# Layer 0's first modulation group: four of its eight steps on TensorE in front of the statistics of x

## The chip, the core and the metric

The kernel runs on one core of a Trainium2 chip. A core has TensorE (PE; its weight loads are listed as PEld), VectorE (DVE), ScalarE (ACT), GpSimd (POOL) and SyncE (SP), which issues most transfers. Each engine takes its own queue of instructions in order and waits on semaphores for the others. The time is the device time of one execution in microseconds, the median of three runs; a profiler's record of one more execution gives the rows below.

## The reference

One inference step of a two-layer backbone (`DEPTH = 2`, model width 1024) for 128 context tokens and 512 latent tokens. Each layer computes a modulation vector from a conditioning vector (one for the context, one for the latent tokens), normalises and modulates x, runs four parallel head groups (gated convolution, chunked spatial gating, latent attention, windowed attention), projects, adds through a gate, and then does the same around a squared-ReLU MLP:

```
mod = silu(c) @ w_ada[l] + b_ada[l]          # six vectors of 1024: shift1, scale1, gate1, shift2, scale2, gate2
h   = rmsnorm(x, norm1) * (1 + scale1) + shift1
y   = mixer(h);  x = x + gate1 * y
x   = x + gate2 * (relu(rmsnorm(x, norm2) * (1 + scale2) + shift2) @ w1) ** 2 @ w2
```

where rmsnorm divides x by the root of its mean square over the 1024 channels. The outputs are the final normed tokens and the context's keys and values of each layer.

## The kernel before, in words

All tokens (640) lie together, channels on partitions: x is one tile of 128 x 8 x 640, block k holding channels 128k to 128k + 127. Weights come from memory as `raw` tiles, and ACT and DVE split each into a high and a low part (`load_unit`: ACT copies L239, DVE subtracts L240, output `hl`). The activations `h` are split likewise (L336, L337), and every product is three matmuls (`mm3`, L248 to L250). The first product is that of `tm_block` (tokens on partitions, weights `in_wt`, PSUM tiles `tm`).

The part in question is `first_modulate`, which makes layer 0's first `h`. Its pieces:

- `broadcast_c` (L159, L161): PE and ACT spread the conditioning vectors `cs` over all partitions into `cb`.
- `norm.start()`: ACT squares x block by block (L266, L269), DVE adds the squares into `ss` (L270). Then `rstd` for each half of the tokens (384 and 256): PE sums over partitions (L290), DVE scales and adds epsilon into `nst` (L293), POOL raises to the power -0.5 (L295), PE spreads the result over the partitions (L297, tile `rb`), ACT copies it to `rbs` (L281).
- The modulation of shift1 and scale1 in natural layout, by `AdaRows`: the first group covers channel blocks 0 to 3 and has eight steps, k = 0 to 7. A step is a transfer of 512 KB (`adan`, from `in_wnat`, L311) and two matmuls of 512 columns onto two rows (`adar`, L198). `finish` copies the rows (ACT, `adas`, L205), transposes them (PE, `adat`, L210) and adds the bias (DVE, `mod`, L213; gains L184). A second group covers blocks 4 and 5 (L327, four transfers from `in_wnat2`, matmuls of 256 columns).
- `ada_tile` for blocks 6 and 7, and for all later modulation vectors: a transfer `adaw` (L171) and two multiply-and-sum instructions on DVE (L174, one with output `junk`, one with output `adaw`).
- DVE multiplies x by `rbs` into `xr` (L319), ACT applies gains and shifts (L334) and copies the high part of `h` (L336), DVE subtracts for the low part (L337).

The tile framework lowers this to one queue for each engine. Within an engine it is free to order instructions by its own estimates of when each is ready and by the program's order as a priority; it also hands out the buffers of a pool by these estimates, so that an `adaw` or `adan` tile can stand in a buffer that an earlier one held, and its transfer then waits for the reader of the earlier one. Layer constants that `layer` asks for at its start are drawn forward into the front: the masks (`wide`, L440, cast to `msk`, L442), a row of norms and sinks (`row`, L444) and from it `nsink` (L446). The first weight splits of `tm_block` are drawn forward too.

Of the kernel before, what the change touches and what calls it, by code (L numbers as in the profile page):

```python
# [56 lines left out]
def step_kernel(ctx, tc, xT, wf, wt, wt3, wo1, wo2, wq, wkvs, wada, wnat, wnat2, vec, rows, fnorm, cvec, cache, kpec,  # L57
# [44 lines left out]
    def ta(shape, s, dt=F32R):  # L102
        return pool_a.tile(shape, dt, tag="a", name=nm(s))

    def tb(shape, s, dt=F32R):
        return pool_b.tile(shape, dt, tag="b", name=nm(s))

    def tp(shape, s):
        return pool_p.tile(shape, F32, tag="p", name=nm(s))
# [10 lines left out]
    def f(ap):  # L120
        return ap.bitcast(F32)
# [20 lines left out]
    def late_consts():  # L142
        nc.sync.dma_start(out=vecs[1], in_=vec[1])
        nc.sync.dma_start(out=fn, in_=fnorm)
# [8 lines left out]
    def broadcast_c():  # L153
        for g in range(2):
            for j in range(2):
                ps = bank("cb")
                for i in range(4):
                    k = 4 * j + i
                    nc.tensor.matmul(ps[:, 128 * i:128 * (i + 1)], lhsT=cs[:, g, k:k + 1].to_broadcast([128, 128]),  # L159
                                     rhs=ident, start=True, stop=True)  # L160
                nc.scalar.copy(cb[:, g, 512 * j:512 * (j + 1)], ps)  # L161
# [6 lines left out]
    def ada_tile(l, ct, pool=None):  # L168

        raw = pool([128, D], "adaw", F32) if pool else rawp.tile([128, D], F32, tag="raw", name=nm("adaw"))  # L170
        nc.sync.dma_start(out=raw, in_=wada[l, ct])  # L171
        junk = bank2("junk").rearrange("p a b -> p (a b)")
        for g in range(2):
            nc.vector.tensor_tensor_reduce(  # L174
                out=raw if g else junk, in0=raw, in1=cb[:, g, :], op0=ALU.mult, op1=ALU.add, scale=1.0,
                scalar=vecs[l][:, V_BADA + ct:V_BADA + ct + 1], accum_out=mods[l][g][:, ct:ct + 1])
        v, k = divmod(ct, KT)
        if v in (1, 4):
            gain(l, v // 4, k, 1)
# [122 lines left out]
    def first_modulate():  # L302

        h = [ta([128, 2, TOK], "h") for _ in range(KT)]
        ar = AdaRows(0, 4)
        norm = Norm()
        broadcast_c()
        norm.start()
        for k in range(KT):
            raw = (tb if k % 2 == 0 or k >= 6 else tt)([128, D], "adan", F32)  # L310
            nc.sync.dma_start(out=raw, in_=wnat[k])  # L311
            ar.step(k, raw)
        ts = [None] * KT
        for i in range(3):
            two = ta([128, 2, TOK], "xr", F32)
            ts[2 * i], ts[2 * i + 1] = two[:, 0, :], two[:, 1, :]
        ts[6], ts[7] = tp([128, TOK], "xr"), tp([128, TOK], "xr")
        for k in range(KT):
            nc.vector.tensor_mul(ts[k], x[:, k, :], norm.rb)  # L319
        ar.finish()  # L320
        for k in (6, 7):
            ada_tile(0, k, tb)
            ada_tile(0, KT + k, tb)
        ar = AdaRows(4, 2)
        for k in range(0, KT, 2):
            raw = tb([128, 2, 512], "adan", F32)
            nc.sync.dma_start(out=raw, in_=wnat2[:, k:k + 2, :])  # L327
            for i in range(2):
                ar.step(k + i, raw[:, i, :])
        ar.finish()  # L330
        for k in K_FIRST:
            t = ts[k]
            for t0, n, g in ((0, LAT, 0), (LAT, CTX, 1)):
                nc.scalar.activation(t[:, t0:t0 + n], t[:, t0:t0 + n], AF.Identity,  # L334
                                     scale=gains[0][g][0][:, k:k + 1], bias=mods[0][g][:, k:k + 1])
            nc.scalar.copy(h[k][:, 0, :], t)  # L336
            nc.vector.tensor_sub(h[k][:, 1, :], t, f(h[k][:, 0, :]))  # L337
        late_consts()
        return h
# [994 lines left out]

    open_phase("mix0", lay=1, pt=3)
    h = first_modulate()
    for l in range(DEPTH):
        if l:
            open_phase(f"mix{l}", lay=1, pt=3)
        norm = Norm()  # L1340
# [147 lines left out]
```

## Time and profile before

| what | value |
|---|---|
| median of 3 runs | 1513.88 us (1511.9 to 1515.99) |
| the profiled execution's own time | 1513.0 us |
| its span | 1510.8 us |
| PE busy | 1461.8 us, 97% |
| DVE busy | 1133.2 us, 75% |
| ACT busy | 694.7 us, 46% |
| first `tm` matmul | 46.74 us after the span's start |

Times in the rows are counted from the span's start. A row with "[5.89 <-DMA row<-in_rows]" says that the engine stood 5.89 us before it, and what released it. The span is 2.2 us shorter than the execution's time. Two successive records of an `adar` matmul of 512 columns belong to one instruction, and so do two records of a `cb` or `rb` matmul.

### The profile page before, as it was taken

Reading aid. Unit: us, or ns where it says so; the run is one execution under the profiler, and the core shown is the slowest. Engines: PE = TensorE matmul, PEld = TensorE weight load, DVE = VectorE, ACT = ScalarE, POOL = GpSimd, SP = SyncE. Lnnn points to the kernel's source line nnn. Section 1 sums busy time; section 2 is a strip of 40 time slices with the busy share of each in tenths; the row PEclk is TensorE's granted clock in tenths of the full one; section 3 lists DMA queues with packets and bytes.
Section 4 is the critical chain, followed back from the end, with each engine's and each line's share of the span. In section 5 each row is a group of like instructions: output and inputs, shape, how many; then the busy total and the mean of one; then the engine's idle time right before and its main releaser. Section 6 shows DMA issues by size and latency. Waiting matters only on the chain.

```text
span 1510.8 us, 24974 instructions
## 1 busy us (share of the span) xinstructions
PE 1461.8 (97%) x9700; PEld 1405.1 (93%) x9700; DVE 1133.2 (75%) x2297; ACT 694.7 (46%) x1469; POOL 79.3 (5%) x103
## 2 busy tenths in 40 slices
PE   6999999999999999999999999999999999999997
PEld 3898989899999999999999998998999999999996
DVE  5998888889977867875477676887977666567656
ACT  4644556746233232233246455775826334324431
POOL 0011102200000000000000121110000000000000
PEclk9999999999999999999999999999999999999998
DMA  9643311324655444443112411022123123222312
GB/s 346 205 153 127 96 56 58 96 87 153 194 161 161 155 144 150 153 153 127 64 49 75 134 43 44 22 71 67 57 78 104 57 84 98 70 70 85 96 45 71
DMA packets 50422, 160.87 MB, mean 106 GB/s; under 512 B 6272, under 2 KB 10368, under 8 KB 50304
## 3 DMA queue, kind: packets, MB, share of 16 engines
q1 hardware_dynamic: 48320, 154.68, 31.8%
q10 hardware_dynamic: 1664, 3.93, 0.7%
q8 instruction: 77, 1.26, 0.3%
q0 software_dynamic: 320, 0.66, 0.2%
q14 instruction: 41, 0.34, 0.1%
HBM read 155.55 MB, written 3.05 MB: 105 GB/s over the span
## 4 chain that ended last, share of the span: by engine, by line
PE 81%; DVE 8%; ACT 5%; issue 2%; POOL 1%; DMA 1%; POOLq 0%; DVEq 0%; ACTq 0%
PE w L250 15%; PE w L249 15%; PE w L248 14%; PE tm L250 2%; PE tm L248 2%; PE tm L249 2%; PE qcd L248 2%; PE qcd L250 2%; PE qcd L249 2%; PE out L248 2%; PE fm L248 2%; PE fm L250 2%; PE fm L249 2%; PE out L249 2%; PE out L250 2%
## 5 line engine op out<-in xcount | busy, mean ns | idle before, releaser
L248 PE MATMUL w<-u,hl 128*128 128x384 f32 (+1 forms) x1024 | 315.8, 309 | 1.9 <-DVE x L428 1.2
L249 PE MATMUL w<-u,hl 128*128 128x384 f32 (+1 forms) x1024 | 315.9, 308 | 0.7 <-DVE u L1231 0.7
L250 PE MATMUL w<-u,hl 128*128 128x384 f32 (+1 forms) x1024 | 315.5, 309 | 0.6 <-DVE hl L240 0.6
L239 ACT CAST hl<-raw 128x1024 fp32r<-128x1024 f32 (+3 forms) x176 | 170.7, 972 | 244.0 <-PE w L250 151.4
L240 DVE TENSOR_TENSOR hl<-raw,hl 128x1024 fp32r<-128x1024 f32 (+3 forms) x176 | 199.4, 1135 | 60.6 <-ACT hl L239 59.8
L428 DVE SCALAR_TENSOR_TENSOR x<-w,mod,x 128x128 f32<-128x128 f32 (+1 forms) x384 | 155.4, 434 | 59.4 <-PE w L250 58.1
L248 PEld LDWEIGHTS w<-u,hl 128*128 128x128 f32 x1024 | 193.3, 189 | 3.0 <-DVE x L428 1.4
L249 PEld LDWEIGHTS w<-u,hl 128*128 128x128 f32 x1024 | 193.6, 189 | 1.0 <-DVE u L1231 1.0
L250 PEld LDWEIGHTS w<-u,hl 128*128 128x128 f32 x1024 | 193.4, 189 | 0.8 <-DVE hl L240 0.8
L249 PE MATMUL w<-h,hl 128*128 128x384 f32 (+1 forms) x576 | 178.8, 311 | 0.7 <-DVE h L369 0.6
L248 PE MATMUL w<-h,hl 128*128 128x384 f32 (+1 forms) x576 | 177.8, 311 | 0.4 <-ACT h L365 0.2
L250 PE MATMUL w<-h,hl 128*128 128x384 f32 (+1 forms) x576 | 178.1, 310 | 0.0
L174 DVE CUSTOM_DVE_ANT_0 junk<-adaw,cb,vec 128x1024 f32<-128x1024 f32 x84 | 108.2, 1289 | 30.6 <-DMA adaw<-in_wada 30.5
L249 PEld LDWEIGHTS w<-h,hl 128*128 128x128 f32 x576 | 109.8, 191 | 1.7 <-DVE h L369 1.5
L248 PEld LDWEIGHTS w<-h,hl 128*128 128x128 f32 x576 | 109.6, 191 | 1.4 <-ACT h L365 1.3
L250 PEld LDWEIGHTS w<-h,hl 128*128 128x128 f32 x576 | 109.8, 191 | 0.2
L174 DVE CUSTOM_DVE_ANT_0 adaw<-adaw,cb,vec 128x1024 f32<-128x1024 f32 x84 | 107.9, 1285 | 0.7
L248 PE MATMUL fm<-h,hl 128*128 128x256 f32 (+1 forms) x288 | 91.5, 318 | 0.0
L249 PE MATMUL fm<-h,hl 128*128 128x256 f32 (+1 forms) x288 | 89.7, 311 | 0.0
L250 PE MATMUL fm<-h,hl 128*128 128x256 f32 (+1 forms) x288 | 89.5, 311 | 0.0
L1176 ACT ACTIVATE rr<-w 128x384 f32<-128x384 f32 (+1 forms) x72 | 31.4, 436 | 101.5 <-PE w L250 101.4
L249 PE MATMUL tm<-hl,h 128*128 128x384 f32 (+1 forms) x240 | 77.3, 322 | 0.6 <-DVE hl L240 0.6
(338 smaller groups left out, 3237.1 us busy)
## 6 DMA issues: line engine op xcount, KB each, us to landing
raw<-in_wf SPq DMA_DIRECT2D x146, 512.0 KB, 3.5
adaw<-in_wada SPq DMA_DIRECT2D x84, 512.0 KB, 3.6
raw<-in_wo SPq DMA_DIRECT2D x24, 384.0 KB, 3.1
adan<-in_wnat SPq DMA_DIRECT2D x12, 512.0 KB, 8.2
raw<-in_wt SPq DMA_DIRECT2D x16, 384.0 KB, 4.0
x<-in_xT ACTq DMA_DIRECT2D x4, 640.0 KB, 7.1
raw<-in_wt SPq DMA_DIRECT2D x8, 288.0 KB, 2.8
raw<-in_wo SPq DMA_DIRECT2D x4, 512.0 KB, 3.6
```

Of the source, the lines that this page charges most:

```text
L174: nc.vector.tensor_tensor_reduce(out=raw if g else junk, in0=raw, in1=cb[:, g, :], op0=ALU.mult, op1=ALU.add, scale=1.0, scalar=vecs[l][:, ...
L239: nc.scalar.copy(hl[:, 0, :n], raw[:, :n])
L240: nc.vector.tensor_sub(hl[:, 1, :n], raw[:, :n], f(hl[:, 0, :n]))
L248: nc.tensor.matmul(out, lhsT=lhs[0], rhs=rhs[0], start=start, stop=False, skip_group_check=more)
L249: nc.tensor.matmul(out, lhsT=lhs[0], rhs=rhs[1], start=False, stop=False, skip_group_check=more)
L250: nc.tensor.matmul(out, lhsT=lhs[1], rhs=rhs[0], start=False, stop=stop, skip_group_check=more)
L428: nc.vector.scalar_tensor_tensor(out=x[:, m, t0:t0 + n], in0=ps[:, t0 - b0:t0 - b0 + n], scalar=mods[l][g][:, gate + m:gate + m + 1], in1= ...
L1176: nc.scalar.activation(r, ps[:, :n], AF.Relu)
```

## The change

The start of the statistics moves from in front of the loop over the first group's eight steps to the place between its fourth and its fifth step. Nothing else is edited; from L308 on every line has a number that is higher by one.

```
         broadcast_c()
-        norm.start()
         for k in range(KT):
+            if k == 4:
+                norm.start()
             raw = (tb if k % 2 == 0 or k >= 6 else tt)([128, D], "adan", F32)
             nc.sync.dma_start(out=raw, in_=wnat[k])
             ar.step(k, raw)
```

The order on PE, from behind `cb` to the transposes, with the lines of before (-) and of after (+). Two matmuls onto `adar_138` are one step of the first group; `rb` L290 are the sums over partitions and `rb` L297 the spreading, once for each half:

```order
-L290 MATMUL rb_209<-ones,ss_139 128x1 x3
-L290 MATMUL rb_220<-ones,ss_139 128x1 x2
-L297 MATMUL rb_209<-ident,nst_213 128x128 x3
-L297 MATMUL rb_220<-ident,nst_223 128x128 x2
-L198 MATMUL adar_138<-adan_229,cs 2x512 x2
+L198 MATMUL adar_138<-adan_176,cs 2x512 x2
+L290 MATMUL rb_225<-ones,ss_139 128x1 x3
+L198 MATMUL adar_138<-adan_245,cs 2x512
+L297 MATMUL rb_225<-ident,nst_229 128x128 x3
+L198 MATMUL adar_138<-adan_245,cs 2x512
+L290 MATMUL rb_236<-ones,ss_139 128x1 x2
+L198 MATMUL adar_138<-adan_249,cs 2x512
```

Before, the statistics stand in front of all eight steps; now four steps stand in front of the sums (the fourth is shown), and the matmuls of steps 4 and 5 stand between the pieces of the statistics.

On DVE, from the last sum of squares on, before. `nst` are the statistics, `xr` the products of x and `rbs`, `hl` the low part of a weight split, `msk` the masks:

```order
L270 TENSOR_TENSOR ss_139<-ss_139,sq_205 128x256
L293 TENSOR_SCALAR nst_213<-rb_209 128x3
L293 TENSOR_SCALAR nst_223<-rb_220 128x2
L446 TENSOR_SCALAR nsink_390<-row_388 128x4
L319 TENSOR_TENSOR xr_261<-x,rbs_208 128x640 x2
```

and after:

```order
L270 TENSOR_TENSOR ss_139<-ss_139,sq_221 128x256
L447 TENSOR_SCALAR nsink_390<-row_388 128x4
L240 TENSOR_TENSOR hl_405<-raw_403,hl_405 128x768
L293 TENSOR_SCALAR nst_229<-rb_225 128x3
L443 CAST msk_386<-wide_384 128x768
L293 TENSOR_SCALAR nst_239<-rb_236 128x2
L240 TENSOR_TENSOR hl_410<-raw_408,hl_410 128x768
L320 TENSOR_TENSOR xr_261<-x,rbs_224 128x640 x2
```

Both `nst` now stand behind `nsink` and the first `hl`, the cast of the masks stands between them, and a second `hl` in front of the first `xr`.

On SP, from the first weights on, with the lines of before (-) and of after (+); `raw` are the weights of `tm_block`, `adaw` the transfers of `ada_tile`, `wide` the masks:

```order
 L237 DMA raw_80_403<-in_wt 128x768
+L171 DMA adaw_51_294<-in_wada 128x1024
+L441 DMA wide_65_384<-in_masks 128x768
+L171 DMA adaw_53_301<-in_wada 128x1024
 L237 DMA raw_82_408<-in_wt 128x768
 L237 DMA raw_84_413<-in_wt 128x768
-L1097 DMA kx_347_2187<-in_rope_q 128x640
-L171 DMA adaw_51_294<-in_wada 128x1024
-L440 DMA wide_65_384<-in_masks 128x768
-L171 DMA adaw_53_301<-in_wada 128x1024
```

Up to the first weights the queue is the same; behind them two `adaw` and the masks go in front of the second and third weights. From the first `tm` matmul on, the order on PE is the same in both programs.

## Rows read from the trace of the kernel before

**Rows 1.** The page, part 1: engine, busy us, share, instructions.
```profile
PE 1461.8 (97%) x9700; PEld 1405.1 (93%) x9700; DVE 1133.2 (75%) x2297; ACT 694.7 (46%) x1469; POOL 79.3 (5%) x103
```

**Rows 2.** Windows: stretch, length, busy us by engine, granted clock, DMA share, GB/s.
```profile
core 0: us, PE busy (x) PEld busy (x) DVE busy (x) ACT busy (x) POOL busy (x), PEclk, DMA share, GB/s
11.50:15.20 3.70, 0.01 (x1) 0.00 (x0) 2.40 (x7) 3.09 (x8) 0.00 (x0) 1.00 1.02 407
17.00:23.40 6.40, 6.01 (x15) 2.81 (x16) 0.76 (x2) 0.85 (x2) 1.02 (x2) 0.50 1.02 371
22.60:46.00 23.40, 20.93 (x69) 5.38 (x67) 22.76 (x43) 11.10 (x18) 0.00 (x0) 0.98 0.96 348
46.00:60.00 14.00, 13.62 (x78) 13.16 (x79) 14.00 (x28) 8.90 (x19) 0.00 (x0) 1.00 0.45 149
60.00:100.00 40.00, 40.00 (x253) 40.00 (x252) 38.44 (x84) 21.89 (x73) 4.45 (x4) 1.00 0.53 169
```

**Rows 3.** The chain that ended last, 0 to 47 us: start, length, what.
```profile
31.59 5.16 DMA adan<-in_wnat
...
36.79 1.46 PE adar L198 x6
...
40.43 5.17 ACT xr L334 x9
...
46.74 0.44 PE tm L248
```

**Rows 4.** Waits of PE, 46 to 110 us: total, times, longest.
```profile
PE adat L210 <- ACT adas L205: 0.8, 1, 0.8
PE sgu L248 <- DVE u L609: 0.5, 1, 0.5
PE tm L248 <- ACT h L336: 0.2, 1, 0.2
```

**Rows 5.** Timeline of the front: start, length, engine, line, tiles, count, idle before.
```profile
5.58 5.93 PE L159 MATMUL cb<-ident,cs 128*128 128x128 f32 x32 [5.58 <-DVE cs L151]
...
15.28 1.28 PE L290 MATMUL rb<-ones,ss 128*128 128x1 f32 x10 [3.77 <-DVE ss L270]
...
16.14 0.16 DVE L293 TENSOR_SCALAR nst<-rb 128x3 f32<-128x3 f32 x1 [0.58 <-PE rb L290]
...
17.39 2.50 PE L297 MATMUL rb<-ident,nst 128*128 128x128 f32 x10 [0.84 <-POOL nst L295]
...
19.82 15.79 PE L198 MATMUL adar<-adan,cs 128*2 128x512 f32 x32
19.93 0.37 ACT L281 COPY rbs<-rb 128x256 f32<-128x256 f32 x1 [0.38 <-PE rb L297]
...
22.64 0.17 DVE L446 TENSOR_SCALAR nsink<-row 128x4 f32<-128x4 f32 x1 [5.89 <-DMA row<-in_rows]
22.72 5.97 DVE L319 TENSOR_TENSOR xr<-x,rbs 128x640 f32<-128x640 f32 x8
...
23.76 0.83 ACT L239 CAST hl<-raw 128x768 fp32r<-128x768 f32 x1 [3.46 <-DMA raw<-in_wt]
...
29.81 0.55 DVE L442 CAST msk<-wide 128x768 bf16<-128x768 f32 x1
...
32.69 0.95 DVE L240 TENSOR_TENSOR hl<-raw,hl 128x768 fp32r<-128x768 f32 x1
...
36.98 1.27 DVE L174 CUSTOM_DVE_ANT_0 adaw<-adaw,cb,vec 128x1024 f32<-128x1024 f32 x1
...
19.82 3.58 PE L198 MATMUL adar<-adan,cs 128*2 128x512 f32 x4
```

**Rows 6.** Transfers: first and fourth of the group, all weights: KB, us to landing.
```profile
adan<-in_wnat SPq DMA_DIRECT2D x1, 512.0 KB, 7.4
4.93 0.33 SPq L311 DMA_DIRECT2D adan<-in_wnat  x1
adan<-in_wnat SPq DMA_DIRECT2D x1, 512.0 KB, 10.0
raw<-in_wf SPq DMA_DIRECT2D x146, 512.0 KB, 3.5
```

More of the change, by code (lines that the diff above doesn't have):

```diff
@@ L307, in first_modulate @@
         broadcast_c()
-        norm.start()
         for k in range(KT):
+            if k == 4:
+                norm.start()
             raw = (tb if k % 2 == 0 or k >= 6 else tt)([128, D], "adan", F32)
```

## The prediction, made before the result was known

> **What bounds the kernel now.** I read the page first: TensorE (PE) is busy 97% of the span and VectorE (DVE) 75% [rows 1]. So a change at the start is worth what it does to the moment at which PE gets its steady work, and to what PE waits for after that. The windows of the front come next: in [rows 2] the reader is to see that DVE is busy 22.76 of 23.40 us from 22.6 to 46.0, all of 46 to 60, and 38.44 of 40.00 us from 60 to 100, while PE is full as well. From 22.6 to 100 us both engines are loaded, and DVE has 0.6 + 0 + 1.6 us left. The chain of waits [rows 3] goes through the second modulation group's transfer, `adar`, and the modulation on ScalarE (ACT) to the first token matmul `tm` at 46.74. And the waits of PE after that [rows 4] hold one wait of 0.5 us for DVE (at the `sgu` matmuls): at about 109 us DVE has no lead over PE. A DVE that falls behind in the front is therefore paid for by PE before 110 us.
>
> The timeline [rows 5] gives the front in order. PE spreads `cs` into `cb` (ends 5.58 + 5.93 = 11.51), then has nothing until `ss` is summed (15.28). The statistics run through DVE `nst`, GpSimd `nst` and PE L297 and end in `rbs` at 19.93 + 0.37 = 20.3. The eight steps of the first group take PE from 19.82 to 35.61. DVE has its `nst` done early (16.14), then stands until `row` lands (22.64), and starts the `xr` multiplies at 22.72; from there it hardly pauses.
>
> **The change part by part.** No operation is added or dropped: 16 `adar` matmuls, the same transfers, the same statistics. What moves is the order, and it moves on three engines.
>
> PE, the four steps. Two `adar` matmuls are one step, each leaves two records. Four records at the low clock took 3.58 us, so 1.79 a matmul; the other 28 took 15.79 - 3.58 = 12.21, so 0.87 a matmul [rows 5]. Eight of them behind `cb` are 7.0 us at the high clock: 11.5 to 18.5. The transfers don't stop them: the first lands at 1.64 + 7.4 = 9.0, the fourth at 4.93 + 10.0 = 14.9 [rows 6], and the fourth's turn is 11.5 + 5.2 = 16.7. Taken by itself this fills 3.8 us of PE's idle time and delays the column sums L290 from 15.28 to 18.5.
>
> DVE, the real cost. In the new order `nst` no longer stands directly behind the sums of `ss`. In front of it stand `nsink` and the first weight split `hl`, and between the two `nst` the cast of the masks; a second `hl` stands in front of `xr`. An engine takes its queue in order: [rows 5] show DVE passing nothing while `nsink` waits for `row`, though `rbs` was there from 20.3. Step by step:
> - `nsink` goes at 22.64, since `row` stands at the same place in SyncE's queue.
> - `hl` needs ACT's copy of the first weights, which starts when they land: 23.76 + 0.83 = 24.6. Then `hl` takes 0.95: 25.5. All of that is ahead of the first `nst`, which before ran at 16.14.
> - From `nst` to L297 it took 17.39 - 16.14 = 1.25, so L297 for half 0 starts at 26.8. Three matmuls: 5.93/16 = 0.37 each at the high clock, 2.50/5 = 0.50 at the low one; 27.9 or 28.3.
> - Behind them PE does the second matmul of step 4 (0.87 or 1.79), two column sums (1.28/5 each, 0.5), and half 1's `nst` follows some 0.2 later: 29.5 or 30.8. The masks are in by then: they and one 512 KB transfer stand behind the weights that land at 23.7, 0.92 MB at 0.41 MB a us [rows 2] are 2.2 us, so 25.9.
> - 1.25 later L297 for half 1 could start, 30.7 or 32.0; one `adar` matmul stands before it and ends at 30.2 or 32.4. Two matmuls and the copy to `rbs` (0.37): 31.9 or 33.8.
> So `xr` starts at 31.9 to 33.8 and not at 22.72: 9.2 to 11.1 us later. Of what DVE did later before, two `hl` and the mask cast are done by then, 2 x 0.95 + 0.55 = 2.45 us. DVE's lag on the same work is 6.7 to 8.6 us.
>
> The clock. In [rows 2] PE has nothing from 11.5 to 15.2 and is then granted 0.50 from 17.0 to 23.4, that is 1.2 GHz, before it returns to 2.4 GHz. After the change PE stands from about 19.9 to 26.8, longer than that, so I take the low clock as likelier for what follows 26.8. The Trainium skill, "TensorE: Matmul & The Clock Gate", section "HAM oscillation — how this bites in real kernels", says that a wait between two groups of matmuls re-throttles PE and the next group starts cold; by it the lag is the 8.6 above. Read the other way, that the four early steps keep PE warm, the lag would be 6.7. The trace agrees with the first for a shorter stop.
>
> ACT and the first `tm`. Eight `xr` take 5.97: 37.9 to 39.8. Behind them stand the transposed shift rows (0.24 in all), one modulation reduction (1.27) and the gains, so the first gains come at about 39.5 to 41.4 against 40.4 before, where ACT starts at 40.43 [rows 3]. Eight of ACT's nine pieces of 5.17 us: 44.1 to 46.0. ACT then wants the gains of channel block 6, five reductions of 1.27 behind the first gains: 45.9 to 47.8, then one piece of 0.5, the copy of the second group 0.5 and the cast of `h` 0.6: `tm` at 47.5 to 49.4, which is 0.8 to 2.7 later than 46.74. The rest of DVE's lag is not gone. It stands behind the front as weight splits and evictions that come later, and PE meets it before 110 us.
>
> What of the lag passes: DVE can shrink its 1.6 us of idle between 60 and 100 us. 6.7 - 1.6 = 5.1 and 8.6 - 1.6 = 7.0; I take the middle, 6.0. Its least is the start of `tm` alone (0.8), its most the whole 8.6 with nothing shrunk, or more if transfers come late (below). From about 110 us on the order on PE is the same as before, and PE is full, so what is lost stays lost.
>
> The sum: the profiled execution took 1513.0 us, its span 1510.8; 1513.0 + 6.0 = 1519.0. The median of the three runs is 1513.88, 0.9 above the profiled one, so I predict 1519.9.
>
> **The rivals.**
> Absorbed. The lag is real, but DVE catches up: only the start of `tm` passes, 0.8 to 2.7, which is 1514.7 to 1516.6. For it: PE waits for DVE only 0.5 us in all between 46 and 110 [rows 4], and much of what DVE does there are modulation vectors that are read only later. Against it: that work stands in DVE's queue in front of the splits that PE does read, and DVE has 1.6 us to give.
>
> Faster. The first group no longer stands behind the statistics. If `nst` ran at 18.5 + 0.9 = 19.4 (L290 to `nst` was 0.86), `rbs` would be there at about 23.5, `xr` would slip by under 1 us, PE would end the group with its remaining four steps at about 28 instead of 35.6, and the chain of [rows 3] would lose up to the 7 us between, less what DVE cannot follow: 1506.5 to 1512. It decides by one thing, whether the first `nst` starts before 20 us. Against it stands the DVE order itself: `hl` in front of `nst` cannot run before 24.6.
>
> Heavier. The third transfer of the second group goes into a buffer that its first transfer used, so it waits until PE has done that one's four matmuls. Step 6 ends at about 33.5 to 36; a landing takes 3.5 [rows 6] to 5.16 [rows 3]: 37 to 41. Four matmuls are half as wide as step matmuls, 4 x 0.44 = 1.8; the third transfer lands 3.5 to 5.2 later, 42.3 to 48, and eight matmuls of 0.44 end at 46 to 51.5. ACT's copy of this group stands in front of the casts of `h`; above it was wanted at 46.4 to 48.3. Up to 4 us come on top: 1522 to 1524.
>
> That the change does not do what it says is no rival: the order shows the steps in front.
>
> **How the numbers follow.** This kernel's measurement tells about 0.3% from no change, 4.5 us: faster is under 1509.3, slower over 1518.4. Forecast (lag passes but for DVE's idle time, 1517.9 to 1521): 0.60. Absorbed: 0.21. Heavier: 0.13. Faster: 0.06. The forecast's low end lies inside the 0.3%, 0.04 of it; so slower is 0.56 + 0.13 = 0.69, same 0.21 + 0.04 = 0.25, faster 0.06. The range goes from 1515.0, which leaves out the fast case and the lightest of the absorbed one, to 1523.5, which leaves out the worst of the heavy one.
>
> **What would show it.** Right: `nsink`, `hl`, then `nst` on DVE at 25.5; PE empty between about 20 and 26.8, a clock of 0.50 after it; `xr` from 32 to 34; `tm` 1 to 3 us later; and one wait of PE for DVE of 2 to 4 us between 60 and 110 us that before does not have. Wrong: an `nst` before 24 us; `xr` before 30; PE without a new wait for DVE behind `tm`; or a later start of `tm` by 5 us and more that is released by the second group's transfer.

## The result, and the profile after

| | median of the runs | runs | ratio to before, 95% interval |
|---|---|---|---|
| before | 1515.04 us (1511.9 to 1516.53) | 8 | |
| after | 1525.8 us (1520.26 to 1529.58) | 8 | 1.0075 [1.0059, 1.0091] |
| predicted | 1519.9 us (1515.0 to 1523.5) | | |

The change costs 0.0075 x 1515 = 11.4 us (8.9 to 13.8); the two medians differ by 10.8. The direction was forecast and the size was not: I took 6.0 us, and the median lies outside the range. The profiled execution of after took 1528.39 us, 2.6 over its median; its span is 1526.5.

The page of after, part 1, answers [rows 1]. The work of DVE is the same to 0.1 us, and PE has 6.6 us more, at a mean granted clock of 0.983 against 0.988:

```profile
PE 1468.4 (96%) x9700; PEld 1408.0 (92%) x9700; DVE 1133.1 (74%) x2297; ACT 694.3 (45%) x1469; POOL 80.3 (5%) x103
```

The windows of after, columns as in [rows 2]:

```profile
11.50:15.20 3.70, 3.70 (x20) 1.78 (x19) 2.40 (x6) 3.34 (x9) 0.00 (x0) 1.00 1.03 412
20.00:26.80 6.80, 1.63 (x8) 0.68 (x8) 1.24 (x4) 0.83 (x1) 0.27 (x1) 0.87 1.03 373
26.80:33.60 6.80, 6.14 (x15) 2.48 (x15) 1.56 (x3) 1.21 (x2) 1.97 (x2) 0.50 0.57 197
60.00:100.00 40.00, 37.67 (x218) 37.29 (x217) 38.24 (x81) 20.43 (x60) 2.78 (x3) 1.00 0.53 156
22.60:46.00 23.40, 16.36 (x52) 5.92 (x52) 13.55 (x25) 8.10 (x13) 2.24 (x2) 0.78 0.70 256
46.00:60.00 14.00, 10.35 (x47) 6.55 (x47) 11.15 (x25) 8.41 (x15) 0.00 (x0) 0.88 0.49 162
```

PE is full where it was empty (11.5 to 15.2), and then has 1.63 of 6.80 us from 20.0 on and a granted clock of 0.50 behind that, 1.2 GHz. DVE's busy time from 22.6 to 46 falls from 22.76 [rows 2] to 13.55, and from 46 to 60 from 14.00 to 11.15. The transfers thin out too: their share of the stretch from 22.6 to 46 falls from 0.96 to 0.70.

The front of after in order of time, as in [rows 5]:

```profile
19.85 0.83 PE L290 MATMUL rb<-ones,ss 128*128 128x1 f32 x6
...
23.50 0.17 DVE L447 TENSOR_SCALAR nsink<-row 128x4 f32<-128x4 f32 x1 [7.68 <-DMA row<-in_rows]
24.48 0.83 ACT L239 CAST hl<-raw 128x768 fp32r<-128x768 f32 x1 [9.29 <-DMA raw<-in_wt]
25.35 0.96 DVE L240 TENSOR_TENSOR hl<-raw,hl 128x768 fp32r<-128x768 f32 x1 [1.68 <-ACT hl L239]
26.22 0.15 DVE L293 TENSOR_SCALAR nst<-rb 128x3 f32<-128x3 f32 x1
...
27.46 1.65 PE L297 MATMUL rb<-ident,nst 128*128 128x128 f32 x6 [5.83 <-POOL nst L295]
29.04 1.87 PE L198 MATMUL adar<-adan,cs 128*2 128x512 f32 x2
...
30.84 1.02 PE L290 MATMUL rb<-ones,ss 128*128 128x1 f32 x4
...
31.78 1.87 PE L198 MATMUL adar<-adan,cs 128*2 128x512 f32 x2
31.89 0.16 DVE L293 TENSOR_SCALAR nst<-rb 128x2 f32<-128x2 f32 x1 [4.57 <-PE rb L290]
...
32.13 1.36 POOL L295 TENSOR_TENSOR nst<-nst,mhalf 128x2 f32<-128x2 f32 x1 [4.72 <-DVE nst L293]
...
33.58 1.22 PE L297 MATMUL rb<-ident,nst 128*128 128x128 f32 x4
...
35.24 5.97 DVE L320 TENSOR_TENSOR xr<-x,rbs 128x640 f32<-128x640 f32 x8 [2.32 <-ACT rbs L281]
...
48.81 5.30 PE L198 MATMUL adar<-adan,cs 128*2 128x256 f32 x16 [2.76 <-DMA adan<-in_wnat]
...
54.15 0.57 ACT L205 COPY adas<-adar 2x512 f32<-2x512 f32 x1 [4.61 <-PE adar L198]
...
55.22 0.17 DVE L213 TENSOR_TENSOR mod<-adat,vec 128x4 f32<-128x4 f32 x1 [2.85 <-PE adat L210]
...
55.40 0.44 PE L248 MATMUL tm<-hl,h 128*128 128x384 f32 x1 [0.22 <-DVE mod L213]
```

The sums over partitions are done at 20.7, and `nst` reads them at 26.22: in between DVE passes `nsink` and `hl`, which wait for transfers. `xr` starts 12.5 us later than at 22.72 [rows 5], and `tm` 8.66 later than at 46.74 [rows 3]. These are the longest of PE's waits from 46 to 125 us of after; in [rows 4] there are 1.5 us in all:

```profile
PE adar L198 <- DMA adan<-in_wnat: 2.8, 1, 2.8
PE tm L248 <- DVE mod L174: 2.3, 1, 2.3
PE sgu L248 <- DVE u L610: 1.0, 2, 0.6
```

The first lies in front of `tm`, the others behind it.

To see what is lost I take one and the same `sgu` matmul of layer 0 in every kernel, behind which waits for DVE add half a us at most: it runs at 106.30 us before and at 118.42 after, 12.1 later (8.7 of them up to `tm`; of the other 3.5, the last two waits above make 2.3 and, in the longer of the two for `u`, 0.6). The windows from 0 to it, first of before, then of after (third busy time is DVE's):

```profile
0.00:106.30 106.30, 93.25 (x498) 74.40 (x498) 87.26 (x183) 56.41 (x141) 7.59 (x14) 0.97 0.69 241
```

```profile
0.00:118.42 118.42, 96.69 (x498) 74.62 (x498) 87.19 (x182) 56.24 (x142) 8.56 (x14) 0.94 0.64 216
```

DVE has the same 87.2 us of work in both; it is idle 106.30 - 87.26 = 19.04 us before and 31.23 after. The 12.2 us between are the whole delay. This is a sum that comes out whatever the cause: on PE the same delay is 96.69 - 93.25 = 3.4 us more of busy time, at a lower clock, and 8.7 us more of idle time. Which engine sets the pace is told only by runs in which one of them is moved alone (below). DVE's waits say where they are: first of before, 15 to 106.3 us, then of after, 15 to 118.42 us (total, times, longest):

```profile
DVE nsink L446 <- DMA row<-in_rows: 5.9, 1, 5.9
DVE cq L499 <- POOL rstd L480: 1.0, 1, 1.0
DVE nst L293 <- PE rb L290: 0.9, 2, 0.6
DVE rstd L588 <- POOL rstd L480: 0.8, 1, 0.8
DVE ckp L536 <- POOL rstd L480: 0.7, 2, 0.4
DVE mod L213 <- PE adat L210: 0.6, 1, 0.6
DVE hl L240 <- ACT hl L239: 0.4, 1, 0.4
```

```profile
DVE nsink L447 <- DMA row<-in_rows: 7.7, 1, 7.7
DVE nst L293 <- PE rb L290: 4.6, 1, 4.6
DVE mod L213 <- PE adat L210: 2.9, 1, 2.9
DVE xr L320 <- ACT rbs L281: 2.3, 1, 2.3
DVE hl L240 <- ACT hl L239: 1.7, 1, 1.7
DVE rstd L589 <- POOL rstd L481: 1.1, 2, 0.6
DVE cq L500 <- POOL rstd L481: 0.7, 1, 0.7
DVE ckp L537 <- POOL rstd L481: 0.7, 2, 0.4
DVE msk L443 <- DMA wide<-in_masks: 0.4, 1, 0.4
```

The rows add up to 10.3 and 22.1 us. Up to `xr` it was 5.9 + 0.9 = 6.8 and is 7.7 + 4.6 + 2.3 + 1.7 + 0.4 = 16.7.

### The profile page after: what moved, and what is told of

Same layout as the page of the kernel before. It is cut to its first block, busy times and chain, and to the rows that moved or that the text cites. A ratio compares the mean times of both kernels' runs of the same rounds, so it can differ in the third digit from the quotient of the medians.

```text
span 1526.5 us, 24971 instructions
## 1 busy us (share of the span) xinstructions
PE 1468.4 (96%) x9700; PEld 1408.0 (92%) x9700; DVE 1133.1 (74%) x2297; ACT 694.3 (45%) x1469; POOL 80.3 (5%) x103
## 5 line engine op out<-in xcount | busy, mean ns | idle before, releaser
L429 DVE SCALAR_TENSOR_TENSOR x<-w,mod,x 128x128 f32<-128x128 f32 (+1 forms) x384 | 155.1, 435 | 58.2 <-PE w L250 57.2
L248 PE MATMUL tm<-hl,h 128*128 128x384 f32 (+1 forms) x240 | 76.3, 323 | 2.7 <-DVE mod L174 2.3
L249 PE MATMUL tm<-hl,h 128*128 128x384 f32 (+1 forms) x240 | 77.3, 322 | 0.6 <-DVE hl L240 0.6
```

Source lines behind the costliest of these rows:

```text
L248: nc.tensor.matmul(out, lhsT=lhs[0], rhs=rhs[0], start=start, stop=False, skip_group_check=more)
L249: nc.tensor.matmul(out, lhsT=lhs[0], rhs=rhs[1], start=False, stop=False, skip_group_check=more)
L429: nc.vector.scalar_tensor_tensor(out=x[:, m, t0:t0 + n], in0=ps[:, t0 - b0:t0 - b0 + n], scalar=mods[l][g][:, gate + m:gate + m + 1], in1= ...
```

## The experiments

Three theories. Theory 1: the order on DVE is the root; what makes DVE stand in the front is lost. Theory 2: the transfers and buffers of the second group cost time of their own. Theory 3: the low clock behind PE's idle stretch is the root. In every case below the ratio is against runs of the kernel before on the same chip; 0.001 is 1.5 us. The times within a kernel are those of one profiled execution. `behind(...)` in a diff keeps instructions of one engine behind another of the same engine; it adds no wait.

**Order on DVE and ACT.** Edit of the first (after is the base; the mask and the sinks likewise):

```
-            us = {i: load_unit(srcs[i], kn * cols) for i in seq}
+            with behind(second nst):
+                us = {i: load_unit(srcs[i], kn * cols) for i in seq}
```

> The changed kernel with its four early steps; on VectorE the negated sinks, the mask's cast and the splits of the first wave's weights stand behind the second nst instead of ahead of it; TensorE's order is that of the changed kernel. If VectorE's order is the root of the loss (theory 1), nst runs within 2 us of the end of the first L290 matmuls (before 21.9 us instead of 26.2), x times its rstd (xr) starts near 26 to 29 us instead of 35.2, the first tm matmul of layer 0 comes before 51 us instead of at 55.4, and the median lies 5 to 11 us under the changed kernel's, at 1515 to 1521. If the buffers of the second group's weights are a cause of their own (theory 2), the first tm stays at 53 us or later, and the time within 3 us of the changed kernel's 1525.8. If TensorE's low clock after the idle stretch is the root (theory 3), the time follows whether the granted clock still drops to 0.5 between 25 and 35 us, whatever the place of nst.

Ratio 1.0029 [1.0015, 1.0043], median 1518.32. `nst` ran at 21.51 us, `tm` at 49.12; the granted clock stayed at 1.0 up to 43 us. What theory 1 forecast came: with the order on PE as in after, 7.0 of the 11.4 us are back (to some 3 us). The low clock went with the order, so this run does not part theory 1 from theory 3. It does answer for SP: two `adaw` and the masks still go in front of the second and third weights here. `xr` came only at 30.60, since ACT's casts of the first weights, which wait for their transfers, stood in front of both copies to `rbs` (25.06 and 29.60 us).

The second edit puts ACT's casts behind the second `rbs` too:

```
-            with behind(second nst):
+            with behind(second nst), behind(second rbs copy):
```

> The kernel with the statistics first (1518.3), and the first wave's casts on ScalarE behind the second copy of rstd (rbs) as well; nothing foreign then stands in the chain L290, nst, pow, L297, rbs. In the kernel with the statistics first a cast that waits for its weights stands ahead of each rbs, and xr starts at 30.6 us. Theory 1, widened to ScalarE: xr starts at 26 to 28 us, the first tm at 46.5 to 48.5 us, the median is 1514 to 1517. What is left over 22.7 us is then the four early steps themselves, 3.2 us. Theory 2 (transfers of the second group): xr early, but the first tm stays within 1 us of 49.1 us, and the time at 1517 to 1520.

Ratio 1.0027 [1.0012, 1.0042]. `xr` started at 26.39 and `tm` at 45.29 us, as theory 1 wants, but the time did not follow: `tm` is 1.45 us *earlier* than before, and the kernel is still 4.1 us (1.8 to 6.4) slower. The timeline of this kernel, PE's waits from 46 to 125 us, and DVE's two longest from 15 to 111.27 us:

```profile
20.23 0.16 DVE L298 TENSOR_SCALAR nst<-rb 128x3 f32<-128x3 f32 x1 [4.69 <-PE rb L295]
...
26.39 5.97 DVE L327 TENSOR_TENSOR xr<-x,rbs 128x640 f32<-128x640 f32 x8
...
45.29 0.44 PE L252 MATMUL tm<-hl,h 128*128 128x384 f32 x1 [0.22 <-ACT h L344]
```

```profile
PE tm L252 <- DVE mod L178: 2.3, 1, 2.3
PE sgu L252 <- DVE u L620: 1.0, 2, 0.6
PE tm L253 <- DVE hl L244: 0.9, 1, 0.9
```

```profile
DVE nst L298 <- PE rb L295: 8.2, 2, 4.7
DVE msk L451 <- DMA wide<-in_masks: 1.7, 1, 1.7
```

PE's start says nothing here; the `sgu` matmul, at 111.27, says it: 5.0 late, with DVE busy 87.34 and idle 23.93 us, 4.9 more than before. Up to `xr` DVE waits 8.2 us for the two `nst` and 1.7 for the masks, 9.9 against 6.8 before. The masks are hardly to blame, since `rbs` was not there before 26.05; it is the four steps that hold the sums back from 15.28 to 19.37. So 3.1 of the 4.9 us lie in front of `xr`; the rest is spread over smaller waits, 1.1 of it more at `mod`.

The third put the sinks, the mask and the first splits behind `xr` as well (`behind(last xr)` on DVE, the casts on ACT left alone):

> As the kernel with the statistics first, but the sinks, the mask and the first splits stand behind the eighth xr on VectorE as well. Theory 1 (VectorE's order): xr starts near 26 us, the first tm comes at 47 to 50 us, and the median is 1514 to 1519. Theory 2 (buffers of the second group): the first tm at 53 us or later and a median over 1522. Theory 3 (clock): as theory 2 if the granted clock is 0.5 in 25 to 35 us, as theory 1 if it is not. The first wave's splits start later here than in any other version; if that counts, TensorE waits for them behind the first tm, by up to 5 us.

Ratio 1.0041 [1.0027, 1.0054]. `xr` at 30.30, behind an `rbs` that stood behind a cast; `tm` at 48.72, then 4 us without a split for PE. The late splits counted, as said.

The same edit on the kernel before:

> The kernel before, no early step, with the sinks, the mask and the first splits behind the eighth xr on VectorE. In the profile before, the second nst stands behind the sinks and the first split. Theory 1: xr starts about 2 us earlier than 22.7 us; the second group then still waits for its weights, so that 0 to 2 us are won: 1511 to 1515, within 0.3% or a little faster. Theory 2 and 3: no change, 1513 to 1517. Slower than 1518 would say that the early splits are needed early, and that VectorE's order is not what lost the time.

Ratio 0.9993 [0.9983, 1.0002]: `xr` at 20.10, `sgu` 1.2 us earlier. Not to be told from no change; in sign as expected. (What the expectation says of the profile before is not so: there both `nst` run by 16.8, ahead of `nsink` at 22.64.)

**The clock.** Six matmuls into the idle stretch (`fill()` writes an unused bank):

```
+            if half == 0:
+                fill()      # 6 x matmul(ps[0:2, :512], lhsT=cs[:, :, 0], rhs=x[:, 0, 0:512])
             for i in range(nt):
                 nc.tensor.matmul(rb[:, 128 * i:128 * (i + 1)],
```

> The changed kernel with six matmuls more (x by a column of the condition, 2x512, result never read) between the first L290 matmuls and the first L297 matmuls, so that TensorE stays busy from 20.6 to about 25.8 us, where it waited for nst; the order of VectorE and ScalarE is that of the changed kernel. Theory 3 (the low clock after the idle stretch is the root): the granted clock stays 1.0 to 40 us, the first tm comes at 47 to 50 us, and 7 us or more of the 10.8 are won back. Theory 1 (VectorE's order): nst still stands at 26.2 us, xr starts at 31 to 33 us, the first tm comes at 51 to 54 us, and 1 to 4 us are won back: 1521 to 1525.

Ratio 1.0075 [1.0053, 1.0096], but the run does not tell what it was made for: the framework had moved three casts ahead of the first `rbs` (32.00) and three splits ahead of the second `nst`, so `xr` started later still (36.93). The clock was 1.0 up to 32 us and nothing was won. With the casts held in their places:

> The changed kernel with the six matmuls more between the first L290 and L297 matmuls, and this time the casts on ScalarE held in the places of the changed kernel (in the earlier one with filler three of them ran ahead of the first rbs, which then came at 32.0 instead of 29.2 us). Theory 3 (clock): the granted clock stays 1.0 to 32 us, xr starts at 31 to 33 us and 5 us or more are won back, a ratio under 1.004. Theory 1: 0 to 3 us are won, 1.0055 to 1.0075.

Ratio 1.0044 [1.0031, 1.0058]. The windows of this kernel against the same two of after:

```profile
20.00:26.80 6.80, 6.43 (x22) 2.04 (x22) 1.76 (x4) 0.83 (x1) 0.88 (x1) 1.00 1.03 381
26.80:33.60 6.80, 6.06 (x23) 1.94 (x22) 3.12 (x5) 3.15 (x5) 1.36 (x1) 1.00 1.03 403
```

With the clock at 1.00, `xr` starts at 31.52 and `sgu` comes at 113.67, DVE idle for 26.25. Useless work on PE wins back 0.0031 x 1515 = 4.7 us, with some 3 us of uncertainty. That lies between the bounds of theories 1 and 3. The clock is no root of its own: the first experiment leaves PE's order as it is and the clock stays high, so the low clock follows from the order on DVE, which makes PE stand. But it is a large part of what that order costs: 4.7 of the 7.0 us, and the difference lies within the uncertainty. Some of it is not the clock: `row` landed 1.2 us earlier in this profile (`nsink` 22.29 against 23.50).

**The second group's transfers.** The first two of its four weights go into the other pool, whose buffers steps 1 and 3 leave early:

```
-            raw = tb([128, 2, 512], "adan", F32)
+            raw = (tt if k < 4 else tb)([128, 2, 512], "adan", F32)
```

> The changed kernel, but the first two of the four second-group weights go into the t tiles, which the first group's second and fourth steps leave free early, and the stream's weights and the mask come after them. VectorE's nst still stands behind the sinks and the first split, but ahead of the mask's cast and the second split. Theory 2 (the second group's transfers): its first two transfers land before 40 us, the last L198 matmul ends by 48 instead of 54.1 us, the first tm comes at 49 to 51 us, and 4 to 7 us are won back: 1519 to 1522. Theory 1: xr still starts after 32 us, and the time stays within 3 us of 1525.8, unless the missing second split brings xr forward.

Ratio 1.0073 [1.0053, 1.0093]: no gain in the time. The second group ended at 44.59 instead of 54.11, and `tm` began at 45.88, better than expected; then PE waited 3.0 us for `h` and 0.7 for a split. This run stays half open: in its profile `sgu` comes 4.6 us earlier than in after, and the six runs' times do not show it. Part of this is on record: behind `sgu` this execution lost another 2.9 us, so that its span ends 10.4 us later than that of before; and `cs` landed 1.6 us earlier in this profile than in that of after (2.77 against 4.38 us), which the edit does not explain.

> The kernel with the clean rstd chain, and the first two second-group weights in the t tiles: both causes taken away at once, four steps early. If theories 1 and 2 together hold the whole loss, the first tm comes at 44 to 47 us and the median is at or under the kernel before: 1510 to 1515. If something else holds part of it (the clock, or the first wave's splits, which come late here), it stays over 1517.

Ratio 1.0038 [1.0022, 1.0054]. `tm` at 39.90, the earliest of all, and then one wait of PE:

```profile
PE tm L253 <- DVE hl L244: 9.5, 1, 9.5
```

DVE was busy 87.76 of the 111.57 us to `sgu`, idle 23.81: the same as with the clean chain alone. Theory 2 alone does not hold: earlier transfers bring PE's start forward and turn into a wait for DVE.

**The number of steps in front** (`if k == 2`, and the call behind the loop):

> Two of the eight steps ahead of the statistics instead of four; on VectorE the first nst then stands behind the sinks and ahead of the first split, the second behind one split. Theory 1: nst is later than before by the sinks' wait only, xr starts at 25 to 29 us, the first tm at 47 to 51 us, the median is 1515 to 1520. Theory 2 (each early step frees a buffer early and draws a later weight into it): the loss goes with the number of steps, half of 10.8 us, 1519 to 1522. Theory 3: the time is that of the kernel before, 1513 to 1517, if the granted clock stays at 1.0 to 27 us, and within 3 us of the changed kernel's if it does not.

> All eight steps ahead of the statistics. On VectorE both nst stand behind the sinks and splits, as in the changed kernel. Theory 1 (loss grows with xr's start): the eighth step's weights land near 28 us and the steps take 14.6 us from 11.5 us on, so that L290 comes at 27 to 29 us, xr at 33 to 38 us; the time is that of the changed kernel within 4 us: ratio 1.005 to 1.010. TensorE is hardly idle in front of 27 us, so that theory 3 (clock after the idle stretch) gives less loss than the changed kernel's, under 1.005. Theory 2 (each early step frees a buffer early): twice the loss, 1.012 to 1.016.

Two steps: 1.0046 [1.0027, 1.0065], `xr` at 31.53, `tm` at 53.39. All eight: 1.0071 [1.0059, 1.0083], `xr` at 38.39, `tm` at 51.06. The loss does not go with the number of steps, as theory 2 has it; two steps cost most of it, since DVE's order changes already there. The low clock came with two steps as well (21.3 to 31.6 us), so that this alone does not part theories 1 and 3. Nor does the run with eight: PE was busy up to 27.3, but then stood 5.12 us for `nst`, and the clock was low from 29.1 to 42.8, longer than in after (25.0 to 35.3). What theory 3 was to show there, a smaller loss for want of a low clock, could not come.

**DVE's lag by itself.** Useless multiplications on DVE in the kernel before, with PE's order left as it was (five, then eleven). The edit also holds `ada_tile` for blocks 6 and 7 and the first splits behind the last `xr`; no run has these holds without the multiplications:

```
+        for k in range(5):
+            ins = nc.vector.tensor_mul(ts[7], x[:, 7, :], norm.rb)
         for k in range(KT):
-            nc.vector.tensor_mul(ts[k], x[:, k, :], norm.rb)
+            with behind(ins):
+                nc.vector.tensor_mul(ts[k], x[:, k, :], norm.rb)
```

> The kernel before, no early step, with five multiplications more (128x640, 0.75 us each, results overwritten) ahead of the first xr on VectorE; the stream's and the first wave's instructions on VectorE stay behind the xr. TensorE, its clock and the statistics are as before. Theory 1 in its narrow form (the work that VectorE must do in the front and layer 0's first steps is the bound; what it idles there is lost): xr starts 3.7 us later, at 26.4 us, as in the kernel with the clean rstd chain (1.0027), and the time is 3 to 4.5 us over the kernel before, ratio 1.002 to 1.003. If TensorE's path is the bound, nothing is lost: ratio 1.000 to 1.001, since TensorE's steps run to 35.6 us anyway.

> As the kernel with five, with eleven multiplications: 8.2 us of VectorE. Theory 1: xr starts at 31 us, and 7 to 9 us are lost, ratio 1.0045 to 1.006; with TensorE's steps untouched. Theory 2 (buffers): the second group's transfers come later only as far as VectorE frees its buffers late, and the loss is more than 9 us, over 1.006. TensorE's path as the bound: under 4 us, under 1.0025.

Ratios 1.0034 [1.002, 1.0048] and 1.0060 [1.0043, 1.0078], which is 5.2 and 9.1 us for 3.7 and 8.2 us of work. With five the low clock up to 110 us lasted as long as before (from 16.4 us on). The window to `sgu` with eleven:

```profile
0.00:116.15 116.15, 96.28 (x497) 75.51 (x497) 95.70 (x193) 56.53 (x142) 7.88 (x14) 0.96 0.65 220
```

DVE is busy 8.4 us more than before and idle 1.4 more, and `sgu` is 9.85 late. No early step is in this kernel and PE's steps end at 35.45 as before: DVE's lag alone, whatever makes it, is paid for in full. This shows the second half of theory 1, that DVE's standing is lost; it does not say by which path, since the second group came later here too (its last matmul ended at 50.32 instead of 45.30).

**Less work for DVE.** Sinks, mask and two `xr` on GpSimd, in the kernel before and in the one with the clean chain:

```
-            nc.vector.tensor_mul(ts[k], x[:, k, :], norm.rb)
+            (nc.gpsimd if k in (4, 5) else nc.vector).tensor_mul(ts[k], x[:, k, :], norm.rb)
```

> The kernel before, no early step; the negated sinks, the masks' cast and two of the eight xr run on GpSimd instead of VectorE, so that VectorE has 0.17 + 0.55 + 1.5 = 2.2 us less to do in the front, and its first xr does not stand behind the sinks (20.3 us instead of 22.7). If VectorE bounds the front in the kernel before too, the sgu matmuls of layer 0 (106.3 us in its profile) come 2 to 4.5 us earlier and the ratio is 0.997 to 0.9985. If TensorE bounds the kernel before, so that VectorE's lag costs but its lead gains nothing, the sgu matmuls stay at 105.5 to 106.5 us and the ratio is 0.999 to 1.001. GpSimd's own times are open; if they are long or slow VectorE down, the ratio is over 1.001.

> The kernel with the clean rstd chain (four steps early, ratio 1.0027), with the same four instructions on GpSimd. VectorE bounds: its 2.2 us less come off, ratio 1.0005 to 1.002, sgu at 108.5 to 110 us instead of 111.3. If the loss that is left in that kernel is not VectorE's (transfers, TensorE's early steps themselves), the ratio stays 1.002 to 1.0035. If the four early steps pay once VectorE is relieved, the ratio is under 1.

1.0006 [0.999, 1.0022] and 1.0029 [1.0013, 1.0046]: nothing won. But DVE was not relieved, as its `xr` of the second kernel show (median and longest, ns):

```profile
L329 DVE TENSOR_TENSOR xr<-x,rbs x6: 812/1056/2158, 26.2 to 33.1; 128x640 f32<-128x640 f32 x6
L329 POOL TENSOR_TENSOR xr<-x,rbs x2: 2071/2090/2109, 27.6 to 29.6; 128x640 f32<-128x640 f32 x2
```

Six of them took 7.66 us beside GpSimd's two, where eight alone took 5.97; and up to `sgu` DVE was busy 88.55 and 87.95 us, against 87.26 before and 87.34 with the clean chain. Whether DVE's lead would gain as its lag costs stays open. No kernel of these beats the one before.

All fourteen, and after, in the order of the delay at `sgu`:

| kernel | first `xr` | `tm` | `sgu` late by | loss by the ratio, us |
|---|---|---|---|---|
| before, statistics and `xr` first | 20.10 | 45.53 | -1.2 | -1.1 |
| before, less work for DVE | 20.35 | 48.79 | 1.7 | 0.9 |
| clean chain, less work for DVE | 26.21 | 46.17 | 4.4 | 4.4 |
| five multiplications | 27.52 | 48.52 | 4.5 | 5.2 |
| clean chain | 26.39 | 45.29 | 5.0 | 4.1 |
| clean chain, second group early | 26.70 | 39.90 | 5.3 | 5.8 |
| statistics first | 30.60 | 49.12 | 6.1 | 4.4 |
| after, filler, casts in place | 31.52 | 49.42 | 7.4 | 6.7 |
| second group in other buffers | 32.89 | 45.88 | 7.6 | 11.1 |
| statistics and `xr` first | 30.30 | 48.72 | 8.3 | 6.2 |
| eleven multiplications | 32.95 | 51.61 | 9.9 | 9.1 |
| two steps | 31.53 | 53.39 | 10.4 | 7.0 |
| eight steps | 38.39 | 51.06 | 10.9 | 10.8 |
| after | 35.24 | 55.40 | 12.1 | 11.4 |
| after, filler | 36.93 | 58.17 | 12.5 | 11.4 |

The losses have 2 to 3 us of uncertainty each. The start of `tm` runs from 39.9 to 58.2 and does not order them; the delay at `sgu` nearly does.

## Why the prediction was wrong

- **PE, the four steps: right.** 7.0 us forecast, 12.89 to 19.92 measured. They began 1.4 later than 11.5, because `cs` landed later in this execution (`cb` at 7.12 us instead of 5.58 [rows 5]); in the sixteen traces it lands between 2.77 and 4.38 us, whatever the kernel. In kernels with late steps that shift is hidden behind the sums of squares (L290 at 15.25 to 15.56 in each); behind early steps it is paid.
- **DVE's order: right, 0.7 late.** `nst` at 26.22 against 25.5, both behind `nsink` and `hl`. The experiments show it as the root: 7.0 to 7.3 us go with the order on DVE and ACT, the low clock with it; 4.1 stay with the four steps.
- **The clock: right.** Low from about 25 us on, within the 5.83 us in which PE stood, and high where filler closed the gap. The Trainium skill, "TensorE: Matmul & The Clock Gate", section "HAM oscillation — how this bites in real kernels", says that a wait between two groups of matmuls leaves the next one cold: by that rule the trace agrees, 0.50 with the gap and 1.00 without.
- **ACT and the first `tm`: wrong.** "`tm` at 47.5 to 49.4" was 55.40. I let ACT's copy of the second group be ready when reached, at 46.4 to 48.3; it ran at 54.15, behind matmuls that waited for the third transfer and ran half at the low clock. This is the mechanism of the rival Heavier, to which I gave 0.13, and one of the signs of being wrong that I had named. It is not what the time hangs on: with the second group early `tm` began 9.5 us sooner than in after, and the ratio was 1.0073 against 1.0075.
- **What of the lag passes: this is the term of the sum that failed.** It was a lag of 6.7 to 8.6, less 1.6, taken as 6.0. By DVE's waits it was 16.7 - 6.8 = 9.9 up to `xr`, since `xr` started 1.4 us after the latest time forecast: 0.7 from transfers that landed later, 0.4 from the two column sums, for which I took 0.5 us at either clock and which held PE from 30.84 to 31.78, and 0.2 from the last L297. (The second `pow` took 1.36 us but cost nothing: PE was on the `adar` matmul in front of L297 until 33.58.) To these come 2.9 - 0.6 = 2.3 us at `mod`, where DVE waited for the late second group; and 0.4 was given back instead of 1.6. In sum 11.8. Step by step from the 6.0: 1.0 because I took the middle of two clocks, though I held the low one likelier and it came; 1.3 for a longer lag; 2.3 for `mod`, which the sum did not have; 1.2 for slack that was none. The 1.6 us of idle time between 60 and 100 us in [rows 2] were no slack: in the rows above, DVE stands there for GpSimd's `rstd` (`cq`, `ckp`, `rstd`: 2.5 us in both kernels), and these waits came again in spite of the lag. The sign that I had named for being right came as well: one wait of PE for DVE between 60 and 110 us, of 2.3 us.
- **The rivals.** Absorbed fell: 0.4 us were given back. Faster fell on the order, as said; and with `nst` at 20.23 the clean chain, near its condition of 20, was no gain either.
- **Behind 110 us.** "What is lost stays lost" held for the order but not quite for the profile: after goes from 12.1 us late at `sgu` to 15.7 at the end of the span. Behind `sgu` it spent some 7 us more at the low clock, which at half speed is about the 3.6 us between. Its runs show the same spread: a span of 1518.4 us at a mean granted clock of 0.989, and of 1527.7 at 0.983. The median stands between.

The order is shown by a run that takes it away, and the low clock with it; the clock by a run that takes it away alone. That the early steps' own 4.1 us are DVE's wait for the sums is argued from its waits and from the two lag runs; no run takes that wait away. How much the late second group costs by itself, and whether the new order on SP has a part in the 4.1, stays open.

## What to carry to other kernels

Where two engines are both nearly full for the next hundred microseconds, write the ledger of the one that is met last: its work up to a fixed instruction is constant, so the waits that a change adds there add up to the delay. Then delay that engine alone in a run, to see that it is the one that counts. Here it was, and an earlier start of the other engine was worth nothing. When statistics are moved, look at what the engine's queue now has in front of them; here one instruction that waited for a transfer held all that followed. Idle time counts as slack only after its releaser has been read.

## What the runs showed of the hardware

- TensorE at the low clock for 10 us can cost a kernel through another engine: the filler matmuls, 5 us of useless work, made this one some 4.7 us faster (to some 3 us).
- GpSimd and DVE held each other up. A `pow` on 128x2 took 0.70 us alone (clean chain, 24.18 us) and 1.36 beside a split on DVE (after, 32.13 us), and an `xr` on DVE up to 2.16 instead of 0.82 us beside one on GpSimd of 2.09. The Trainium skill, "SBUF — State Buffer", section "SBUF: two separate sides", says that GpSimd and a DVE instruction with two inputs in SBUF share a pair of ports, which one holds for a whole instruction while the other blocks; by that rule the trace agrees, the longest `xr` being about as long as one of GpSimd's.
